# A softmax's division moved from the probabilities to the attention output, as a row that goes through DRAM

## The chip, the core and the metric

The kernel runs on one core of one Trainium2 chip, in one launch. The core has five engines with queues of their own: TensorE (PE: matmul; PEld: its weight loads), VectorE (DVE), ScalarE (ACT), GpSimd (POOL) and SyncE (SP), on whose queue nearly all DMAs are issued. An engine runs its queue in order; between engines, semaphores say when an operand is there or a buffer free. The metric is the time of one execution in microseconds, the median of several runs.

## The reference, cut to what matters

One decoder layer for a sequence of 512 tokens and a width of 1024: a SwiGLU block, then gated linear attention ("GLA") beside forgetting attention ("FoX"), then another SwiGLU block. The change lies in FoX: 16 heads of 64 columns, a causal softmax over 512 keys with a decay F in the logits.

```python
logf = jax.nn.log_sigmoid((f_b + b_f).astype(f32)).transpose(0, 2, 1)
F = jnp.cumsum(logf, axis=-1)
    s = jnp.einsum('bhqd,bhkd->bhqk', qi, k).astype(jnp.float32) * scale
    s = s + Fi[..., None] - F[:, :, None, :]
    s = jnp.where(kpos[None, :] <= qpos[:, None], s, -jnp.inf)
    p = jax.nn.softmax(s, axis=-1)
    return jnp.einsum('bhqk,bhkd->bhqd', p.astype(v.dtype), v)
merged = jax.nn.sigmoid(gate_a) * (o_a @ w_pa) + jax.nn.sigmoid(gate_b) * (o_b @ w_pb)
```

All of it is float32. The kernel gets this precision by cutting operands into two rounded halves (hi and lo, type fp32r) and adding three products of halves.

## The kernel before

The FoX stage works on eight pairs of heads (p = 0 to 7; e is the head within a pair; the two heads take 64 partitions each where a tile holds both). The loop over p (L990 to L1009) is written in this order: fox_soft(p), fox_scores(p + 1), transposes of p (fox_turn), output product of p (fox_out), and then evacuate(), which makes the operands of a later pair's scores out of matrix products. In a pair:

- fox_scores: SP loads a row of F for each head, broadcast to 128 partitions (L872); GpSimd prepares the decay and the mask (L876, L878); TensorE makes, for each of four blocks of 128 queries and each head, a score product in two parts (L890, L891); VectorE adds the decay and takes the row maxima (L894).
- fox_soft: the maxima are negated (L901), ScalarE takes the exponentials with their row sums (L903), VectorE the sums' reciprocals (L905), and each block of queries is multiplied by its reciprocal, one for each partition (L907: four instructions a head, of 128 to 512 columns).
- fox_turn: TensorE transposes the probabilities in blocks of 128 x 128 (L919), ScalarE copies them out (L921).
- fox_out: 16 products with the values (L930) give the output in PSUM with the 64 columns of each head on the partitions and the 512 queries in the columns; hilo (L208 to L210) rounds it into the high half on ScalarE (L209) and subtracts for the low half on VectorE (L210).
- evacuate: qk_parts (L743 to L763) makes the halves of queries and keys for the scores of a later pair out of two finished products: on ScalarE L755, L757 and L761, on VectorE L756, L758 and L760, for each head.

Beside that, TensorE is kept busy with the steps of Fill (L660 to L763): projections of the layer's input (L203), whose weights come in blocks. A block is loaded by SP into one of four buffers "raw" (L151), rounded on ScalarE into a buffer "whi" (L166), and its remainder is taken on VectorE into a buffer "wlo" (L167). There are five buffers each of whi and wlo, used in turn: the cast into one waits for the last product that read what was in it. The load of a step is written four steps ahead of its products.

The order of each engine's queue isn't the written one: a scheduler of the framework sorts all instructions by its own estimates. So an edit in one place can move instructions of other lines.

Of the kernel before, what the change touches and what calls it, by code (L numbers as in the profile page):

```python
# [8 lines left out]
F32 = mybir.dt.float32  # L9
# [4 lines left out]
ALU = mybir.AluOpType  # L14

P = 128
T = 512
D = 1024
NT = T // P
# [21 lines left out]
def tile_hybrid_layer(  # L41
# [4 lines left out]
    nc = tc.nc  # L46
# [6 lines left out]
    dr = ctx.enter_context(tc.tile_pool(name="dr", bufs=1, space=bass.MemoryType.DRAM))  # L53
# [5 lines left out]
    def nm(s):  # L59
        uid[0] += 1  # L60
        return f"{s}_{uid[0]}"

    def unit(dt=F32, shape=(P, 512)):
        return sb.tile(list(shape), dt, tag="u", bufs=NU, name=nm("u"))

    def tmp(shape=(P, 512), dt=F32):
        return sb.tile(list(shape), dt, tag="t2", bufs=NTMP, name=nm("t2"))
# [4 lines left out]
    def acc(shape=(P, 512)):  # L72
        return pm.tile(list(shape), F32, tag="mm", name=nm("mm"))
# [134 lines left out]
    def hilo(hi, lo, src, eng=None):  # L208
        nc.scalar.copy(hi, src)  # L209
        (eng or nc.vector).tensor_tensor(lo, src, hi.bitcast(F32), ALU.subtract)  # L210
# [447 lines left out]
    halves = (slice(0, 64), slice(64, P))  # L658
# [199 lines left out]
    def s_at(u, i):  # L858

        return (u[1][:, 384:512], u[2], u[1][:, 0:384], u[0])[i]  # L860

    def p_at(u, j):

        return (u[0], u[1][:, 0:384], u[2], u[1][:, 384:512])[j]
# [30 lines left out]
                                               ALU.add, ALU.max, nmx[e][:, i:i + 1])  # L895
        return S, nmx, rs

    def fox_soft(state):
        S, nmx, rs = state
        for e in range(2):  # L900
            nc.vector.tensor_scalar(nmx[e], nmx[e], -1.0, None, ALU.mult)  # L901
            for i in range(NT):
                nc.scalar.activation(s_at(S[e], i), s_at(S[e], i), AF.Exp, bias=nmx[e][:, i:i + 1],  # L903
                                     accum_out=rs[e][:, i:i + 1])
            nc.vector.reciprocal(rs[e], rs[e])  # L905
            for i in range(NT):
                nc.vector.tensor_scalar(s_at(S[e], i), s_at(S[e], i), rs[e][:, i:i + 1], None, ALU.mult)  # L907

    def fox_turn(state):
        S = state[0]  # L910
# [14 lines left out]
    def fox_out(p, PT):  # L925
        po = acc()
        for j in range(NT):
            for e in range(2):
                h = 2 * p + e
                nc.tensor.matmul(po[64 * e:64 * e + 64, j * P:T], vb[j][h // 8][:, (h % 8) * 64:(h % 8 + 1) * 64],  # L930
                                 p_at(PT[e], j), start=j == 0, stop=j == NT - 1)
        o = (unit(F32R), unit(F32R))
        hilo(o[0], o[1], po)
        ob.append(o)

    def sig_tanh(ps):
# [43 lines left out]
    def evacuate():  # L980
        while late:
            late.pop(0)()
# [4 lines left out]
    st = [fox_scores(0, *fqk[0], lambda: F.run(1))]  # L987
    evacuate()
    F.run(1)
    for p in range(8):  # L990
        fox_soft(st[p])
        if p < 7:
            F.run(1)
            st.append(fox_scores(p + 1, *fqk[p + 1], lambda: F.run(1) if p == 6 else None))
        if p < 6:
            F.until(marks[p + 2] - 1)
        else:
            F.run(2 if p == 6 else 3)
        PT = fox_turn(st[p])
        F.run(1)  # L1000
        fox_out(p, PT)
        evacuate()
        if p == 5:
            ra2 = tmp()
            tc.keep_in_program_order(nc.sync.dma_start(ra2[0:16], w_a2))
            wa2, fill_wa2 = stacked((0, 1, 0))
            fill_wa2(ra2[0:16])
        if p < 7:
            F.run(1)  # L1009
# [281 lines left out]
```

## Time and profile before

| | us |
|---|---|
| median of three runs (1421.54 to 1423.88) | 1421.57 |
| the profiled execution | 1425.45 |
| its span in the trace | 1423.4 |
| TensorE matmuls busy in the span | 1361.4 (96%) |
| VectorE busy | 910.4 (64%) |
| ScalarE busy | 595.5 (42%) |
| GpSimd busy | 206.6 (15%) |

The mean granted clock of TensorE over the span is 0.992 of full speed. The FoX stage lies between 480 and 660 us of the span. Busy time says how long an engine works, not whether anyone waits for it: the views that answer this are the waits of an engine (who ended its idle time), the engines in order of time, and the chain of work that ended last. In lines of the timeline, the bracket at the end gives the idle time just ahead and the instruction that ended it.

### The profile page before, as it was taken

To read this page: it belongs to the slowest core of one execution; us is meant where nothing else is said; L and a number is where in the kernel's file an instruction comes from. 1 tells how busy PE (TensorE), PEld (TensorE's weight loads), DVE (VectorE), ACT (ScalarE), POOL (GpSimd) and SP (SyncE) were. 2 spreads that over 40 slices of the span, in tenths; PEclk is the share of its full clock that TensorE was granted. 3 is DMA by queue.
4 is the path that set the end of the run, shared out by engine and by line. 5 is a ranking of instruction groups with operands and counts; after the bars stand their busy time and mean duration, and the time that the engine had idled before them with its cause. 6 is when DMAs were issued, how large, how long until landed. Compare 5 with 4: busy or idle time off the path is not lost.

```text
span 1423.4 us, 19497 instructions
## 1 busy us (share of the span) xinstructions
PE 1361.4 (96%) x7485; PEld 1146.4 (81%) x7485; DVE 910.4 (64%) x1410; ACT 595.5 (42%) x1026; POOL 206.6 (15%) x328
## 2 busy tenths in 40 slices
PE   4899999999999999999999999999999999999998
PEld 3699899888877867777888887787878999987886
DVE  6888678685266689762745546538577877866222
ACT  6444444223154476663723333332355444433221
POOL 6200000000050644340110202100050000000001
PEclk8999999999999999999999999999999999999999
DMA  9413233597336755322232232125631332346431
GB/s 322 150 62 112 82 104 110 179 290 265 103 107 182 226 163 167 94 71 78 90 117 75 60 87 62 60 74 160 210 119 45 119 119 75 104 134 196 130 118 59
DMA packets 164089, 180.84 MB, mean 127 GB/s; under 512 B 9226, under 2 KB 128118, under 8 KB 163996
## 3 DMA queue, kind: packets, MB, share of 16 engines
q1 hardware_dynamic: 163564, 178.81, 40.2%
q8 instruction: 59, 0.97, 0.3%
q10 hardware_dynamic: 432, 0.79, 0.2%
q14 instruction: 34, 0.28, 0.1%
HBM read 173.25 MB, written 6.32 MB: 126 GB/s over the span
## 4 chain that ended last, share of the span: by engine, by line
PE 71%; DVE 15%; DMA 6%; ACT 3%; issue 3%; POOL 2%; SPq 0%; DVEq 0%; POOLq 0%; ACTq 0%
PE mm L203 47%; PE mm L394 11%; PE mm L456 7%; DVE wlo L167 5%; DMA raw<-in_w_gu_dram 3%; PE aux L1108 1%; DMA u<-in_w_ada_dram 1%; DVE u L210 1%; DVE t L473 1%; ACT whi L166 1%; DMA raw<-in_w_ada_dram 1%; PE aux L919 1%; PE mm L930 1%; DVE u L907 1%; DVE raw L444 1%
## 5 line engine op out<-in xcount | busy, mean ns | idle before, releaser
L166 ACT CAST whi<-raw 128x1024 fp32r<-128x1024 f32 x262 | 273.3, 1050 | 516.7 <-PE mm L203 261.8
L167 DVE TENSOR_TENSOR wlo<-raw,whi 128x1024 fp32r<-128x1024 f32 x260 | 323.1, 1248 | 247.6 <-ACT whi L166 244.1
L203 PE MATMUL mm<-whi,u 128*128 128x512 f32 x1216 | 392.1, 398 | 1.7 <-DVE t L367 1.5
L203 PE MATMUL mm<-u,whi 128*128 128x512 f32 x896 | 289.9, 402 | 0.8 <-DVE u L1135 0.8
L456 PE MATMUL mm<-u,whi 128*128 128x256 f32 x1568 | 279.3, 281 | 10.6 <-DVE t L473 10.6
L203 PEld LDWEIGHTS mm<-whi,u 128*128 128x128 f32 x1216 | 228.2, 188 | 54.9 <-ACT u L209 1.7
L456 PEld LDWEIGHTS mm<-u,whi 128*128 128x128 f32 x1568 | 239.8, 188 | 13.9 <-DVE t L473 13.2
L203 PE MATMUL mm<-wlo,u 128*128 128x512 f32 x608 | 240.3, 395 | 1.0 <-DVE wlo L167 1.0
L456 PE MATMUL mm<-u,wlo 128*128 128x256 f32 x784 | 219.0, 280 | 0.0
L203 PEld LDWEIGHTS mm<-u,whi 128*128 128x128 f32 x896 | 167.3, 189 | 39.3 <-DVE u L1135 1.2
L394 PE MATMUL mm<-u,whi 128*128 128x512 f32 (+1 forms) x576 | 168.5, 380 | 11.0 <-ACT u L209 9.9
L203 PE MATMUL mm<-u,wlo 128*128 128x512 f32 x448 | 178.6, 399 | 0.0
L456 PEld LDWEIGHTS mm<-u,wlo 128*128 128x128 f32 x784 | 147.3, 188 | 0.0
L203 PEld LDWEIGHTS mm<-wlo,u 128*128 128x128 f32 x608 | 114.2, 188 | 28.8 <-DVE wlo L167 1.3
L394 PEld LDWEIGHTS mm<-u,whi 128*128 128x128 f32 x576 | 105.4, 191 | 35.1 <-ACT u L209 13.2
L394 PE MATMUL mm<-u,wlo 128*128 128x512 f32 (+1 forms) x288 | 105.4, 375 | 0.0
L203 PEld LDWEIGHTS mm<-u,wlo 128*128 128x128 f32 x448 | 84.7, 189 | 19.7
L321 POOL TENSOR_SCALAR sm<-ss 128x1 f32<-128x1 f32 x12 | 2.3, 190 | 642.9 <-ACT jk L328 642.9
L224 DVE SCALAR_TENSOR_TENSOR t<-raw,csil,t 128x512 f32<-128x512 f32 x98 | 74.0, 756 | 10.0 <-DMA raw<-in_w_ada_dram 7.8
L394 PEld LDWEIGHTS mm<-u,wlo 128*128 128x128 f32 x288 | 55.3, 192 | 10.3
L209 ACT CAST u<-t 128x256 fp32r<-128x256 f32 (+1 forms) x94 | 40.8, 454 | 43.5 <-DVE t L523 23.0
L876 POOL TENSOR_SCALAR u<-t,Ft 128x128 f32<-128x128 f32 (+1 forms) x64 | 44.3, 702 | 90.5 <-DMA t<-Fd 67.1
(197 smaller groups left out, 1381.1 us busy)
## 6 DMA issues: line engine op xcount, KB each, us to landing
raw<-in_w_gu_dram SPq DMA_DIRECT2D x88, 512.0 KB, 3.9
raw<-in_w_in_dram SPq DMA_DIRECT2D x64, 512.0 KB, 3.8
raw<-in_w_dn_dram SPq DMA_DIRECT2D x44, 512.0 KB, 5.2
raw<-in_w_ada_dram SPq DMA_DIRECT2D x64, 256.0 KB, 3.7
raw<-in_w_ada_dram SPq DMA_DIRECT2D x24, 512.0 KB, 5.2
u<-in_w_ada_dram SPq DMA_DIRECT2D x32, 256.0 KB, 6.3
raw<-in_w_in_dram SPq DMA_DIRECT2D x20, 256.0 KB, 2.8
t<-Fd SPq DMA_DIRECT2D x16, 256.0 KB, 5.1
```

Of the source, the lines that this page charges most:

```text
L166: nc.scalar.copy(hi, raw)
L167: (eng or nc.vector).tensor_tensor(lo, raw, hi.bitcast(F32), ALU.subtract)
L203: nc.tensor.matmul(ps, a[i], b[j], start=first and n == 0, stop=last and n == 2)
L209: nc.scalar.copy(hi, src)
L210: (eng or nc.vector).tensor_tensor(lo, src, hi.bitcast(F32), ALU.subtract)
L224: nc.vector.scalar_tensor_tensor(a, raw[:, j, :], csil[:, k:k + 1], a, ALU.mult, ALU.add)
L394: nc.tensor.matmul(p_[:, ts], w_[k][i][:, cs], hs[k][e][:, ts], start=ks[0] == 0 and n == 0, stop=ks[-1] == KD - 1 and n == 3 * len(ks) - 1)
L444: nc.vector.tensor_tensor(a12, a12, a11, ALU.subtract)
L456: nc.tensor.matmul(ps[:, j], *((h_[:, js], w_) if self.turned else (w_[:, js], h_)), start=first and k + j + m == 0, stop=k == 3 and m == ...
L473: nc.vector.tensor_tensor(o, ps, a, ALU.add)
L876: nc.gpsimd.tensor_scalar(s_at(s, i), fb[:, 0:n], -1.0, Ft[:, i, h:h + 1], ALU.mult, ALU.add)
L907: nc.vector.tensor_scalar(s_at(S[e], i), s_at(S[e], i), rs[e][:, i:i + 1], None, ALU.mult)
```

## The change

The exponentials are no longer multiplied by the reciprocals (L907 is gone). The transposes and the products with the values take them as they are. The division is made on the output: there, a query is a column, so the reciprocals are needed as a row. They are stored to DRAM as one row of 512 for each head (512 pieces of four bytes, out of a tile of 128 x 4) and loaded again, broadcast to the 64 partitions of that head. VectorE multiplies the product in PSUM by this tile and writes the result over it in SBUF (L940 of after); hilo then reads this.

```diff
--- before.py
+++ after.py
@@ -895,7 +895,10 @@
                                                ALU.add, ALU.max, nmx[e][:, i:i + 1])
         return S, nmx, rs
 
-    def fox_soft(state):
+    Rd = dr.tile([16, T], F32, name="Rd")
+    rows_ = []
+
+    def fox_soft(p, state):
         S, nmx, rs = state
         for e in range(2):
             nc.vector.tensor_scalar(nmx[e], nmx[e], -1.0, None, ALU.mult)
@@ -903,8 +906,12 @@
                 nc.scalar.activation(s_at(S[e], i), s_at(S[e], i), AF.Exp, bias=nmx[e][:, i:i + 1],
                                      accum_out=rs[e][:, i:i + 1])
             nc.vector.reciprocal(rs[e], rs[e])
-            for i in range(NT):
-                nc.vector.tensor_scalar(s_at(S[e], i), s_at(S[e], i), rs[e][:, i:i + 1], None, ALU.mult)
+
+            nc.sync.dma_start(Rd[2 * p + e].rearrange("(i p) -> p i", p=P), rs[e])
+        row = unit()
+        for e in range(2):
+            nc.sync.dma_start(row[halves[e]], Rd[2 * p + e].partition_broadcast(64))
+        rows_.append(row)
 
     def fox_turn(state):
         S = state[0]
@@ -930,7 +937,8 @@
                 nc.tensor.matmul(po[64 * e:64 * e + 64, j * P:T], vb[j][h // 8][:, (h % 8) * 64:(h % 8 + 1) * 64],
                                  p_at(PT[e], j), start=j == 0, stop=j == NT - 1)
         o = (unit(F32R), unit(F32R))
-        hilo(o[0], o[1], po)
+        nc.vector.tensor_tensor(rows_[p], po, rows_[p], ALU.mult)
+        hilo(o[0], o[1], rows_[p])
         ob.append(o)
 
     def sig_tanh(ps):
@@ -988,7 +996,7 @@
     evacuate()
     F.run(1)
     for p in range(8):
-        fox_soft(st[p])
+        fox_soft(p, st[p])
         if p < 7:
             F.run(1)
             st.append(fox_scores(p + 1, *fqk[p + 1], lambda: F.run(1) if p == 6 else None))
```

With that the scheduler's order changes from about 480 us to the end of the FoX stage; outside it, TensorE's order is the same. Three places follow, of before and of after. In the names, a number at the end marks one buffer's use; line numbers of after are three to eight higher (L921 is L928, L905 is L908).

SP, in pair 0, before: the F row of a later head (t) between weight loads (raw).

```order
L268 DMA raw_4892<-in_w_ada_dram 128x2x256 x2
L268 DMA raw_4897<-in_w_ada_dram 128x2x256 x2
L268 DMA raw_4902<-in_w_ada_dram 128x2x256 x2
L872 DMA t_842_4729<-Fd 128x512
L268 DMA raw_4907<-in_w_ada_dram 128x2x256 x2
L151 DMA raw_4946<-in_w_in_dram 128x8x128
L151 DMA raw_5026<-in_w_in_dram 128x8x128
```

The same in after:

```order
L268 DMA raw_4899<-in_w_ada_dram 128x2x256 x2
L910 DMA Rd<-sm_4349 128x4x1
L910 DMA Rd<-sm_4364 128x4x1
L913 DMA u_4478<-Rd 64x512
L872 DMA t_844_4725<-Fd 128x512
L913 DMA u_4478<-Rd 64x512
L268 DMA raw_4904<-in_w_ada_dram 128x2x256 x2
L151 DMA raw_4940<-in_w_in_dram 128x8x128
L151 DMA raw_5020<-in_w_in_dram 128x8x128
```

The two stores, which wait for the reciprocals of pair 0, and the two loads of the row (u_4478) have come between the weight loads; t_844 is issued between the two loads of the row.

ScalarE, ahead of the scores of pair 4, before: whi casts, the output's rounding (L209), then for each head L755, L757, L761.

```order
L166 CAST whi_5411<-raw_5409 128x1024
L209 CAST u_5105<-mm_5096 128x512
L755 CAST u_5111<-mm_4913 64x512
L757 ACTIVATE u_5109<-mm_4912 64x512
L761 COPY u_5111<-u_5113 64x512
L755 CAST u_5112<-mm_4913 64x512
L757 ACTIVATE u_5110<-mm_4912 64x512
L761 COPY u_5112<-u_5114 64x512
L166 CAST whi_5491<-raw_5489 128x1024
```

The same in after:

```order
L166 CAST whi_5401<-raw_5399 128x1024
L209 CAST u_5099<-u_4937 128x512
L755 CAST u_5106<-mm_4910 64x512
L757 ACTIVATE u_5104<-mm_4909 64x512
L761 COPY u_5106<-u_5108 64x512
L755 CAST u_5107<-mm_4910 64x512
L166 CAST whi_5481<-raw_5479 128x1024
L757 ACTIVATE u_5105<-mm_4909 64x512
L761 COPY u_5107<-u_5109 64x512
L928 COPY u_5263<-aux_5266 128x512
L928 COPY u_5264<-aux_5272 128x512
```

The last cast of a weight block (whi_5491 before, whi_5481 after) has moved from behind both heads' operands to ahead of the second head's L757, and two copies of transposes (L928) stand behind.

VectorE at the same place, before:

```order
L905 RECIPROCAL sm_4993<-sm_4993 128x4
L907 TENSOR_SCALAR u_4982<-u_4982,sm_4993 128x128
L907 TENSOR_SCALAR u_4983<-u_4983,sm_4993 128x256
L907 TENSOR_SCALAR u_4982<-u_4982,sm_4993 128x384
L907 TENSOR_SCALAR u_4981<-u_4981,sm_4993 128x512
L167 TENSOR_TENSOR wlo_5242<-raw_5239,whi_5241 128x1024
L210 TENSOR_TENSOR u_5106<-mm_5096,u_5105 128x512
L756 TENSOR_TENSOR u_5113<-mm_4913,u_5111 64x512
L758 SCALAR_TENSOR_TENSOR u_5109<-mm_4912,u_5109 64x512
L760 COPY u_5113<-u_5111 64x512
L286 SCALAR_TENSOR_TENSOR scc_3823<-aux_5129,cols 128x2
L287 TENSOR_TENSOR shc_3822<-aux_5129,cols 128x2
```

And in after:

```order
L167 TENSOR_TENSOR wlo_5234<-raw_5231,whi_5233 128x1024
L940 TENSOR_TENSOR u_4937<-mm_5090,u_4937 128x512
L286 SCALAR_TENSOR_TENSOR scc_3823<-aux_5124,cols 128x2
L287 TENSOR_TENSOR shc_3822<-aux_5124,cols 128x2
L288 TENSOR_TENSOR scc_3823<-scc_3823,cols 128x2
L167 TENSOR_TENSOR wlo_5402<-raw_5399,whi_5401 128x1024
L210 TENSOR_TENSOR u_5100<-u_4937,u_5099 128x512
L756 TENSOR_TENSOR u_5108<-mm_4910,u_5106 64x512
L758 SCALAR_TENSOR_TENSOR u_5104<-mm_4909,u_5104 64x512
L760 COPY u_5108<-u_5106 64x512
L756 TENSOR_TENSOR u_5109<-mm_4910,u_5107 64x512
L760 COPY u_5109<-u_5107 64x512
```

The four multiplies are gone, the new one (L940) stands behind the first weight remainder, and two more remainders stand between: wlo_5402 ahead of L210, wlo_5482, of the block whose cast moved, ahead of the second head's L758 (the row that follows is L758 with u_5105).

TensorE at the scores of pair 4, before (u_5111 to u_5114 and u_5109, u_5110 are the operands made above):

```order
L890 MATMUL mm_5207<-u_5111,u_5109 128x128
L203 MATMUL mm_5163<-u_3616,whi_4948 128x512
L891 MATMUL mm_5207<-u_5113,u_5109 128x128
L203 MATMUL mm_5163<-u_3617,whi_4948 128x512
L203 MATMUL mm_5163<-u_3616,wlo_4949 128x512
L203 MATMUL mm_5163<-u_3618,whi_4948 128x512
L203 MATMUL mm_5163<-u_3619,whi_4948 128x512
L203 MATMUL mm_5163<-u_3618,wlo_4949 128x512
L203 MATMUL mm_5163<-u_3620,whi_4948 128x512
L890 MATMUL mm_5210<-u_5112,u_5110 128x128
L891 MATMUL mm_5210<-u_5114,u_5110 128x128
L890 MATMUL mm_5215<-u_5111,u_5109 128x256
```

And in after (u_5104 to u_5109 are the operands):

```order
L203 MATMUL mm_5155<-u_3621,whi_4942 128x512
L203 MATMUL mm_5155<-u_3620,wlo_4943 128x512
L890 MATMUL mm_5199<-u_5106,u_5104 128x128
L891 MATMUL mm_5199<-u_5108,u_5104 128x128
L926 MATMUL aux_5266<-ident,u_4961 128x128
L926 MATMUL aux_5266<-ident,u_4962 128x128
L926 MATMUL aux_5266<-ident,u_4961 128x128
L926 MATMUL aux_5266<-ident,u_4960 128x128
L926 MATMUL aux_5272<-ident,u_4962 128x128
L926 MATMUL aux_5272<-ident,u_4961 128x128
L926 MATMUL aux_5272<-ident,u_4960 128x128 x2
L890 MATMUL mm_5202<-u_5107,u_5105 128x128
```

Before, products of L203 stand between the first and the second head's first scores; after, they have all been done ahead of the scores, the last read of whi_4942 being the first row (whi_5481 takes its buffer), and eight transposes (L926) of the pair before stand between.

## Rows read from the trace of the kernel before

**Rows 1.** Stretches: us, PE, PEld, DVE, ACT, POOL busy (instructions), granted clock, DMA share, GB/s.

```profile
480.00:660.00 180.00, 174.82 (x906) 134.55 (x905) 127.95 (x334) 109.94 (x256) 71.96 (x134) 0.99 0.42 125
620.00:630.00 10.00, 9.71 (x38) 7.96 (x39) 7.00 (x22) 3.29 (x9) 2.55 (x4) 0.83 0.33 100
```

**Rows 2.** TensorE's waits, 480 to 660 us: us in total, times, longest.

```profile
PE mm L890 <- DVE u L758: 4.0, 3, 1.8
PE mm L890 <- DVE sm L894: 0.5, 1, 0.5
PE mm L891 <- DVE u L760: 0.4, 2, 0.2
```

**Rows 3.** Timeline of PE: start, us, operation, idle ahead and its releaser.

```profile
499.81 0.30 PE L890 MATMUL mm<-u,u 128*128 128x128 f32 x1 [1.19 <-DVE u L758]
...
620.11 0.30 PE L890 MATMUL mm<-u,u 128*128 128x128 f32 x1 [1.82 <-DVE u L758]
```

**Rows 4.** Groups by line and shape, L907: busy us, mean ns, idle ahead.

```profile
L907 DVE TENSOR_SCALAR u<-u,sm 128x128 f32<-128x128 f32 x16 | 5.0, 312 | 0.4
L907 DVE TENSOR_SCALAR u<-u,sm 128x256 f32<-128x256 f32 x16 | 6.8, 426 | 0.0
L907 DVE TENSOR_SCALAR u<-u,sm 128x384 f32<-128x384 f32 x16 | 8.1, 509 | 0.0
L907 DVE TENSOR_SCALAR u<-u,sm 128x512 f32<-128x512 f32 x16 | 8.9, 559 | 0.0
```

**Rows 5.** Chain that ended last, 480 to 680 us, shares by line.

```profile
by line: PE mm L203 44.8%; PE aux L919 5.8%; PE mm L930 5.8%; DVE u L907 5.1%; issue 4.2%; PE mm L890 3.6%; PE mm L891 3.6%; ACT u L903 3.1%; DVE u L758 2.4%; DVE u L756 2.3%; DVE u L894 2.2%; DVE wlo L167 2.2%; ACT u L921 1.5%; DVE u L210 
```

**Rows 6.** Timeline of DVE ahead of the scores of pair 3.

```profile
533.54 2.25 DVE L907 TENSOR_SCALAR u<-u,sm 128x128 f32<-128x128 f32 x4
535.71 1.48 DVE L167 TENSOR_TENSOR wlo<-raw,whi 128x1024 fp32r<-128x1024 f32 x1
...
537.72 0.67 DVE L756 TENSOR_TENSOR u<-mm,u 64x512 fp32r<-64x512 f32 x1
```

**Rows 7.** Timeline of ACT in the same place.

```profile
527.23 1.07 ACT L921 COPY u<-aux 128x512 f32<-128x512 f32 x2
...
533.17 1.06 ACT L166 CAST whi<-raw 128x1024 fp32r<-128x1024 f32 x1
```

**Rows 8.** Groups by line and shape: L758 and L167 of 480 to 660, L209 of the span.

```profile
L758 DVE SCALAR_TENSOR_TENSOR u<-mm,u 64x512 fp32r<-64x512 f32 x16 | 11.0, 688 | 0.8 <-ACT u L757 0.4
...
L167 DVE TENSOR_TENSOR wlo<-raw,whi 128x1024 fp32r<-128x1024 f32 x20 | 25.5, 1280 | 17.9 <-ACT whi L166 16.5 <-DMA raw<-in_w_in_dram 1.4
...
L209 ACT CAST u<-u 128x512 fp32r<-128x512 f32 x20 | 11.9, 618 | 32.7 <-DVE u L605 23.7 <-DVE u L407 4.1 <-DVE u L405 2.8
```

**Rows 9.** Timeline of PE: output products of pairs 0 and 1.

```profile
510.80 2.37 PE L930 MATMUL mm<-u,u 128*64 128x512 f32 x16
...
531.63 2.37 PE L930 MATMUL mm<-u,u 128*64 128x512 f32 x16
```

**Rows 10.** Timeline of ACT behind the operands of pair 4.

```profile
558.55 0.62 ACT L761 CAST u<-u 64x512 fp32r<-64x512 f32 x1 [0.31 <-DVE u L756]
562.03 1.06 ACT L166 CAST whi<-raw 128x1024 fp32r<-128x1024 f32 x1 [2.87 <-PE mm L203]
```

**Rows 11.** Chain that ended last: eight transposes.

```profile
526.70 0.87 PE aux L919 x8
```

**Rows 12.** DMA issues: operation, count, KB each, median us to landing.

```profile
t<-Fd SPq DMA_DIRECT2D x16, 256.0 KB, 5.1
...
Fd<-u SPq DMA_DIRECT2D x1, 32.0 KB, 2.5
...
sm<-in_b_f_dram SPq DMA_DIRECT2D x1, 0.1 KB, 3.3
```

**Rows 13.** Timeline of DVE in pair 0.

```profile
502.66 0.17 DVE L905 RECIPROCAL sm<-sm 128x4 f32<-128x4 f32 x1
```

**Rows 14.** Timeline of DVE ahead of the scores of pair 7.

```profile
617.24 1.28 DVE L167 TENSOR_TENSOR wlo<-raw,whi 128x1024 fp32r<-128x1024 f32 x1
```

## The prediction

> **What bounds the kernel now.** I read the table of stretches first. In the stretch that the change touches, 480 to 660 us, TensorE is busy 174.82 of 180 us, VectorE 127.95, ScalarE 109.94 [rows 1]. So TensorE sets the end there, and work that leaves VectorE is worth only what TensorE waits for. The second view, TensorE's waits in that stretch, names these: 4.0 us in three waits for the query parts that L758 makes, 0.5 us for a row maximum of L894, 0.4 us for L760 [rows 2]. Together that is 4.9 us out of 180. The third view, TensorE in order of time, shows the two largest: 1.19 us at 499.81 (scores of pair 1) and 1.82 us at 620.11 (pair 7) [rows 3], both times the second head's first score product, which waits for its operands; the last of the three is then 4.0 - 1.19 - 1.82 = 1.0 us, at pair 3. Behind the wait at 620.11 the granted clock of 620 to 630 us is 0.83 instead of 1.00 [rows 1], part of the time on the lower of its two levels, 1.2 instead of 2.4 GHz; 10 us at 0.83 cost 10 x 0.17 = 1.7 us, if the wait is what brought the clock down. So the whole change can return at most 4.9 + 1.7 = 6.6 us, however much it takes from VectorE.
>
> **The change part by part.** (1) The 64 multiplies of L907 leave: 16 each of four widths, 5.0 + 6.8 + 8.1 + 8.9 = 28.8 us of VectorE [rows 4]. They stand between the softmax's reciprocals and the transposes, and the chain of waits does carry L907 for 5.1% of its 200 us from 480 to 680 [rows 5], some 10 us. But that chain names whatever was last at each step, with TensorE's own queue close behind it; by [rows 2] TensorE sees at most 4.9 us of it.
>
> (2) What decides are the scores of a pair, since their operands (L755 to L761) are made right after the attention output of the pair two before is cut into its two halves. At pair 3 the trace shows this chain on VectorE: four multiplies of L907 from 533.54, a weight remainder (L167) at 535.71, the output's remainder (L210), L756 at 537.72 [rows 6]. After, this begins with L167. Its rounded half is cast on ScalarE from 533.17 for 1.06 us [rows 7], behind the exponentials; L167 takes 1.28 [rows 8], to 535.5. Then the new multiply by the row, which no row shows; its nearest is L758, which also reads a matrix product 512 columns wide and takes 688 ns [rows 8]: 0.7, to 536.2. Only then ScalarE rounds the output (618 ns for one from SBUF [rows 8]), to 536.8, a cast that ran beside L907 before; L210 with 0.7, and L756 starts at 537.5 instead of 537.72. So **28.8 us less of VectorE moves this chain by only 0.2 us**, since the multiply and the cast now stand in a row in it. Bounds: if L167 came behind L756, this would start 534.0 + 0.7 + 0.6 + 0.7 = 536.0, 1.7 us sooner, 534.0 being the end of the output's product (531.63 + 2.37 [rows 9]); if a second weight remainder stands between, as in the order's rows of VectorE before the scores of pair 4, it starts 1.28 - 0.6 - 0.2 = 0.5 us later than now. In all eight new multiplies cost 8 x 0.69 = 5.5 us, so VectorE's whole busy time falls by 28.8 - 5.5 = 23.3 us.
>
> (3) The transposes no longer wait for L907. In the order of after, the first eight transposes of the odd pairs therefore stand between the scores of the following pair, and two of ScalarE's copies, 1.07 us at 527.23 among the exponentials [rows 7], go ahead of these, into time in which ScalarE waits. The exponentials of pairs 2, 4 and 6, and with them the chain of (2) for the scores of pairs 3, 5 and 7, then end 1.1 us earlier. At pair 3 this makes 0.2 + 1.1 = 1.3 us, within the bound of 1.7 that the output's product sets: more than the 1.0 us of waiting.
>
> (4) The same move brings a new coupling, shown by the order's rows for ScalarE, VectorE and TensorE at the scores of pair 4. The cast of a later weight block, whi, has moved ahead of L757 of the second head. It fills a slot that is free only when TensorE has done the last product that reads the old block, and in after this product stands right before the scores. In before that cast stood behind L761: it starts at 562.03 after 2.87 us of waiting for a product of L203, and nobody needs it, the L761 ahead of it having started at 558.55 [rows 10]. After, the second head's scores wait for TensorE's own product, then the cast of 1.06 [rows 10], then a remainder L167 of 1.28, which stands ahead of L758 on VectorE, then L758, 0.69 [rows 8]: 3.0 us. What covers it on TensorE are the eight transposes, 0.87 us [rows 11], and some 0.4 us of short products: 1.3. New wait at pair 4: 3.0 - 1.3 = **1.7 us**. Before the scores of pair 2 the cast alone stands ahead of L757: 1.06 + 0.62 (as L761 [rows 10]) + 0.69 - 1.3 = 1.1 us; before those of pair 6 it stands ahead of L761 only: 1.06 + 0.62 - 1.3 = 0.4 us. Bounds: 0, where the slot is free earlier, to twice these.
>
> (5) The rows' way through DRAM: 16 stores of 128 x 4 and 16 loads of 64 x 512 on SP's queue, none of which exists before. Bounds for a store from the nearest rows: 2.5 us (Fd<-u) to 3.3 (sm<-in_b_f, sixteen four-byte pieces) [rows 12]; for a load, half of t<-Fd's 256 KB, 2.5, to its whole 5.1 [rows 12]. The tightest is pair 0: its second reciprocal is done at 502.66 + 0.17 = 502.83 [rows 13], so the row is there between 507.8 and 511.2. It is needed when the output product of pair 0 ends, 510.80 + 2.37 = 513.2 [rows 9]. Cover 2.0 to 5.4 us, so its cost is nothing; I take the small cover, since the pieces are small. The other pairs' reciprocals come a pair ahead of their output. Waiting on SP's queue behind a store are t<-Fd and weight loads; of the idle time before L167 only 1.4 us is put down to a weight load [rows 8], so a store of a few us ahead is hidden. Without the cover a late row holds the multiply, and behind it on VectorE the next pair's reciprocal, L167, L210 and L756 to L760, for which TensorE's scores wait.
>
> The Trainium skill's page "DMA: Bandwidth & Descriptors", section "Specifications", asks for at least 512 bytes a transfer, below which the DMA engine reads, modifies and writes. Each store here is 512 pieces of four bytes, so by it (5) would be the place to lose. No row of before shows such a store; the sixteen four-byte pieces that it shows are reads. The sum doesn't use the rule; what it would do is the last rival.
>
> (6) Pair 7. A remainder of L167 (617.24, 1.28 us [rows 14]) leaves from between the two heads' L756, and (3) moves the chain up; the lateness of pairs 4 and 6 uses up part of the wait of 1.82 at 620.11 in any case. It shrinks by 0.5 to 1.8 us; I take 1.2.
>
> **The sum on TensorE's path.** Pair 1's wait at 499.81 has no L907 ahead of it: 0. Pair 2: now 0.5 + 0.2 for L894 and L760 [rows 2], after 1.1: +0.4. Pair 3: -1.0. Pair 4: +1.7. Pair 5, which doesn't wait now: 0. Pair 6: +0.4. Pair 7: -1.2. Row: 0. Together 0.4 - 1.0 + 1.7 + 0.4 - 1.2 = **+0.3 us**. The profiled execution took 1425.45 us and becomes 1425.75; it is 3.9 us above the median of the runs, and the difference carries over: 1421.57 + 0.3, **1421.9 us**. About 0.2%, 2.8 us, is what a measurement of this kernel can tell from no change.
>
> **Rivals.** *Relief reaches TensorE.* If (4) is smaller than I read it, because the cast's slot comes free early enough, all waits of [rows 2] but that at 499.81 go, 3.7 us, and the clock's 1.7 too: -5.4, 1416.2 us. For it: the chain carries 10 us of L907 [rows 5]. Against it: the order shows the new wait. *The new coupling costs more.* Each wait of 1.7 us can bring the clock down as at 620 us: if those of pairs 2 and 4 each cost 1.7 on top, and pair 7 gives back only 0.5: 0.3 + 3.4 + 0.7 = +4.4, 1426.0 us. For it: 1.82 us of idling was followed by 0.83. Against it: 1.19 us at 499.81 was not, the whole stretch being at 0.99 [rows 1]. *The row comes late.* If 512 four-byte stores take over 3.3 + 2.0 = 5.3 us to land, pair 0 waits; at three times the 3.3, 9.9, the row is 4.6 us late, the scores of pair 2 start that much later, and pair 3's may lose 2 more: +5 to +7, 1427 to 1429 us. It decides from 5.3 us on. *The multiplies don't go away*: excluded, no L907 is in the order of after.
>
> **How the numbers follow.** Forecast 0.47 (1418.7 to 1424.4, likeliest 1421.9); relief 0.19; coupling 0.20; late row 0.14. So faster by over 0.2% 0.19, within it 0.47, slower 0.34. The range goes from 1417.0 (most of the first rival lies below) to 1428.5 (part of the last lies above), which leaves out 0.2.
>
> **What would show it.** VectorE's busy time of the whole span falls by some 23 us, TensorE's doesn't change. Among TensorE's waits there is one of 1 to 2 us for L758 at the scores of pairs 2 and 4 each, none at pair 3, a short one at pair 7. The new multiply waits for no transfer at any pair or, if the last rival is right, for microseconds at pair 0; the store's time to landing says which. The forecast is wrong if the clock drops at more than one place, if the new multiply takes much over 0.7 us, or if the stage's end shifts by more than 3 us.

## The result, and the profile after

The changed kernel takes **1441.62 us**, median of four runs (1439.33 to 1443.64), against 1421.71 us for the kernel before on the same chip: ratio 1.0135, 95% interval 1.0122 to 1.0148. It is 19.9 us slower; 1421.9 us was forecast, with a range of 1417.0 to 1428.5. The profiled execution took 1442.24 us, with a span of 1440.5.

VectorE did lose its work. In the page's first part, VectorE falls from 910.4 to 893.9 us, 16.5 less; added up instruction by instruction it is 22.7 less (the busy time counts the overlap of neighbouring instructions once):

```profile
PE 1370.6 (95%) x7485; PEld 1153.6 (80%) x7485; DVE 893.9 (62%) x1354; ACT 596.5 (41%) x1026; POOL 204.7 (14%) x328
```

The stretch of the FoX stage has grown. Stretches as in [rows 1] (us, PE, PEld, DVE, ACT, POOL busy, granted clock, DMA share, GB/s):

```profile
480.00:700.00 220.00, 201.33 (x996) 156.02 (x995) 118.80 (x287) 122.54 (x270) 69.83 (x134) 0.95 0.54 120
520.00:540.00 20.00, 16.13 (x81) 12.39 (x82) 11.71 (x30) 12.50 (x31) 3.79 (x8) 0.83 0.72 83
540.00:560.00 20.00, 17.10 (x76) 13.93 (x75) 13.36 (x33) 9.29 (x21) 8.36 (x16) 0.83 0.72 171
560.00:580.00 20.00, 14.26 (x75) 10.72 (x74) 12.96 (x27) 10.84 (x22) 5.58 (x8) 0.89 0.65 115
```

Before, TensorE was busy 174.82 of the 180 us of [rows 1], at 0.99. Now there are three stretches of 20 us with 14 to 17 us of TensorE, at 0.83 to 0.89. Look at the two columns at the end: from 520 to 540 us the DMA engines are busy for 0.72 of the time and move 83 GB/s; from 540 to 560 us the same 0.72 moves 171. Busy engines that move little are the first sign.

The waits of TensorE, 480 to 700 us (in total, times, longest), answer [rows 2]:

```profile
PE mm L890 <- DVE u L758: 16.8, 9, 6.3
PE mm L890 <- DVE u L760: 0.9, 1, 0.9
PE mm L890 <- ACT u L761: 0.7, 1, 0.7
```

4.0 us in three waits have become 16.8 in nine. The two longest, in the timeline of TensorE (compare [rows 3]):

```profile
523.71 0.45 PE L890 MATMUL mm<-u,u 128*128 128x128 f32 x1 [6.31 <-DVE u L758]
...
577.93 0.45 PE L890 MATMUL mm<-u,u 128*128 128x128 f32 x1 [4.23 <-DVE u L758]
```

They stand at the scores of pairs 2 and 4. Ahead of the first stands VectorE's queue, here its timeline in pair 0:

```profile
501.14 0.18 DVE L908 RECIPROCAL sm<-sm 128x4 f32<-128x4 f32 x1 [2.00 <-ACT u L906]
...
516.64 0.69 DVE L940 TENSOR_TENSOR u<-mm,u 128x512 f32<-128x512 f32 x1 [5.31 <-DMA u<-Rd]
```

And ScalarE's timeline in the same place:

```profile
519.35 1.04 ACT L166 CAST whi<-raw 128x1024 fp32r<-128x1024 f32 x1 [7.52 <-DMA raw<-in_w_in_dram]
```

The reciprocal of pair 0's second head is done at 501.3, but the new multiply starts only at 516.64, after 5.31 us of waiting for the row (u<-Rd): 501.3, a store's 10.5 us and a load's 5.1 (both below) make 516.9. And ScalarE's cast waits as well: it has been idle 7.52 us, and what it waits for is a weight block.

Of the two, the cast ends last. The multiply is done at 517.33, but the remainder of that block stands between it and L210, L756 and L758 on VectorE, and it waits for the cast:

```profile
520.43 1.23 DVE L167 TENSOR_TENSOR wlo<-raw,whi 128x1024 fp32r<-128x1024 f32 x1 [1.82 <-ACT whi L166]
```

Why the block is late, SP's queue shows:

```profile
499.16 2.55 SPq L910 DMA_DIRECT2D Rd<-sm  x2
508.27 0.51 SPq L913 DMA_DIRECT2D u<-Rd  x1
...
512.54 1.04 SPq L151 DMA_DIRECT2D raw<-in_w_in_dram  x2
```

From 501.71 to 508.27 SP issues nothing: the row's load (L913) is next in its queue and waits for the store. The weight load behind it is issued at 512.54 and lands 6.7 us later. Between 480 and 700 us the row loads wait on SP's queue for their stores eight times, 32.0 us in all, up to 7.3. So a late store delays more than its own row: it delays whatever stands behind the row's load.

The groups of these two, 480 to 700 us (busy, mean, idle ahead and what ended it):

```profile
L166 ACT CAST whi<-raw 128x1024 fp32r<-128x1024 f32 x23 | 24.0, 1050 | 37.5 <-DMA raw<-in_w_in_dram 15.4 <-PE mm L203 12.6 <-issue 4.1
...
L940 DVE TENSOR_TENSOR u<-mm,u 128x512 f32<-128x512 f32 x8 | 5.5, 685 | 7.8 <-DMA u<-Rd 5.5 <-PE mm L937 2.3
```

15.4 us of the casts' idle time ends with a weight load. In before there is no such part in that group's row:

```profile
L166 ACT CAST whi<-raw 128x1024 fp32r<-128x1024 f32 x26 | 26.8, 1054 | 28.6 <-PE mm L203 18.0 <-issue 5.6 <-PE mm L890 3.9
```

The DMA issues (count, KB each, median us to landing) point at the cause; they answer [rows 12]:

```profile
u<-Rd SPq DMA_DIRECT2D x16, 128.0 KB, 5.1
...
Rd<-sm SPq DMA_DIRECT2D x16, 2.0 KB, 10.5
...
Fd<-u SPq DMA_DIRECT2D x1, 32.0 KB, 2.7
```

A store of 2 KB in 512 pieces takes **10.5 us** to land, a store of 32 KB 2.7. I had bounded it at 2.5 to 3.3.

### The profile page after: what moved, and what is told of

Its sections match the earlier page's. It is cut to its first block, busy times and chain, and to the rows that moved or that the text cites. A ratio compares the mean times of both kernels' runs of the same rounds, so it can differ in the third digit from the quotient of the medians.

```text
span 1440.5 us, 19524 instructions
## 1 busy us (share of the span) xinstructions
PE 1370.6 (95%) x7485; PEld 1153.6 (80%) x7485; DVE 893.9 (62%) x1354; ACT 596.5 (41%) x1026; POOL 204.7 (14%) x328
## 4 chain that ended last, share of the span: by engine, by line
PE 66%; DVE 15%; DMA 9%; ACT 4%; issue 3%; POOL 2%; SPq 0%; DVEq 0%; POOLq 0%; ACTq 0%
PE mm L203 42%; PE mm L394 11%; PE mm L456 8%; DVE wlo L167 4%; DMA raw<-in_w_in_dram 3%; DMA raw<-in_w_gu_dram 3%; PE aux L1116 1%; ACT whi L166 1%; DMA raw<-in_w_dn_dram 1%; DMA raw<-in_w_ada_dram 1%; DVE u L210 1%; DVE t L473 1%; DVE t L224 1%; DMA Rd<-sm 1%; DVE raw L444 1%
## 5 line engine op out<-in xcount | busy, mean ns | idle before, releaser
L167 DVE TENSOR_TENSOR wlo<-raw,whi 128x1024 fp32r<-128x1024 f32 x260 | 323.2, 1248 | 257.9 <-ACT whi L166 254.5
L203 PE MATMUL mm<-whi,u 128*128 128x512 f32 x1216 | 391.4, 397 | 1.7 <-ACT u L209 1.5
L203 PE MATMUL mm<-u,whi 128*128 128x512 f32 x896 | 288.3, 401 | 0.8 <-DVE u L1143 0.8
L203 PEld LDWEIGHTS mm<-whi,u 128*128 128x128 f32 x1216 | 228.2, 188 | 55.7 <-ACT u L209 1.7
L203 PE MATMUL mm<-wlo,u 128*128 128x512 f32 x608 | 241.4, 397 | 1.6 <-DVE wlo L167 1.6
L203 PEld LDWEIGHTS mm<-u,whi 128*128 128x128 f32 x896 | 166.9, 189 | 39.6 <-DVE u L1143 1.2
L203 PE MATMUL mm<-u,wlo 128*128 128x512 f32 x448 | 178.6, 399 | 0.0
L203 PEld LDWEIGHTS mm<-wlo,u 128*128 128x128 f32 x608 | 114.2, 188 | 29.3 <-DVE wlo L167 2.8
L203 PEld LDWEIGHTS mm<-u,wlo 128*128 128x128 f32 x448 | 84.8, 189 | 19.8
L394 PEld LDWEIGHTS mm<-u,wlo 128*128 128x128 f32 x288 | 55.9, 194 | 10.6
L209 ACT CAST u<-t 128x256 fp32r<-128x256 f32 (+1 forms) x94 | 40.8, 454 | 43.5 <-DVE t L523 22.9
L876 POOL TENSOR_SCALAR u<-t,Ft 128x128 f32<-128x128 f32 (+1 forms) x64 | 40.6, 645 | 121.3 <-DMA t<-Fd 102.2
```

The lines of the kernel that those rows point to most:

```text
L167: (eng or nc.vector).tensor_tensor(lo, raw, hi.bitcast(F32), ALU.subtract)
L203: nc.tensor.matmul(ps, a[i], b[j], start=first and n == 0, stop=last and n == 2)
L394: nc.tensor.matmul(p_[:, ts], w_[k][i][:, cs], hs[k][e][:, ts], start=ks[0] == 0 and n == 0, stop=ks[-1] == KD - 1 and n == 3 * len(ks) - 1)
L876: nc.gpsimd.tensor_scalar(s_at(s, i), fb[:, 0:n], -1.0, Ft[:, i, h:h + 1], ALU.mult, ALU.add)
```

## The experiments

The question was which part costs the 19.9 us: the new order of the queues, the row that comes late, or the stores themselves, by what they do to other transfers. Each kernel was run four to ten times and is compared with the kernel before, run on the same chip beside it (median 1423.49 us for e1 to e4, 1423.42 for e5 to e8, 1422.65 for e9 to e12). The last column is the median of the landings that the trace recorded.

| kernel | median us | over before | ratio, 95% interval | store's landing us |
|---|---|---|---|---|
| after | 1441.62 | +19.9 | 1.0135 (1.0122 to 1.0148) | 10.5 |
| e1_no_trip | 1423.53 | 0.0 | 1.0003 (0.9993 to 1.0013) | no store |
| e2_stores_only | 1436.46 | +13.0 | 1.0096 (1.0072 to 1.0120) | 9.9 |
| e3_before_stores | 1443.14 | +19.7 | 1.0139 (1.0122 to 1.0155) | 10.4 |
| e4_16byte_pieces | 1426.65 | +3.2 | 1.0023 (1.0010 to 1.0036) | 2.5 |
| e5_128_pieces | 1429.62 | +6.2 | 1.0043 (1.0027 to 1.0058) | 8.6 |
| e6_spread | 1423.41 | 0.0 | 1.0005 (0.9993 to 1.0018) | 2.1 |
| e7_other_queue | 1441.97 | +18.6 | 1.0129 (1.0111 to 1.0148) | 10.6 |
| e8_pinned_no_trip | 1424.78 | +1.4 | 1.0013 (1.0000 to 1.0026) | no store |
| e9_turned_row | 1433.64 | +11.0 | 1.0069 (1.0046 to 1.0092) | not recorded |
| e10_spacing_16 | 1423.30 | +0.7 | 1.0011 (0.9998 to 1.0025) | 3.0 |
| e11_trip_spread | 1426.42 | +3.8 | 1.0029 (1.0015 to 1.0043) | 2.5 |
| e12_trip_close | 1439.52 | +16.9 | 1.0123 (1.0095 to 1.0151) | 12.3 |

### Without the way through DRAM: e1_no_trip

```diff
-            nc.sync.dma_start(Rd[2 * p + e].rearrange("(i p) -> p i", p=P), rs[e])
-        row = unit()
-        for e in range(2):
-            nc.sync.dma_start(row[halves[e]], Rd[2 * p + e].partition_broadcast(64))
-        rows_.append(row)
...
-        nc.vector.tensor_tensor(rows_[p], po, rows_[p], ALU.mult)
+        rows_.append(unit())
+        nc.vector.tensor_tensor(rows_[p].rearrange("q (i c) -> q i c", c=P), po.rearrange("q (i c) -> q i c", c=P),
+                                ones.unsqueeze(1).to_broadcast([P, NT, P]), ALU.mult)
```

> The change without its way through DRAM: no stores, no row loads; the output product is multiplied by a tile of ones that is there all along (the division is left out). The multiplies L907 are gone and the queues' order is that of after but for small shifts: the later cast whi stands ahead of the second head's L757 or L761 at pairs 2, 4 and 6. Theory 'trip' (the row's transfers cost the time): within 3 us of before, 1419 to 1425 us. Theory 'order' (the new coupling of the cast and the chain of multiply and cast cost it): 1435 us or more, with waits for L758 of several us at pairs 2 and 4.

Measured: 1423.53 us, as before. Its order is that of after but for small shifts. So the change without its transfers costs and gains nothing that these times can tell, and the theory "order" has fallen. TensorE's waits, 480 to 700 us:

```profile
PE mm L890 <- DVE u L758: 3.7, 3, 2.3
PE mm L890 <- ACT u L761: 2.2, 3, 0.9
PE aux L921 <- ACT u L923: 0.5, 2, 0.3
```

The timeline of TensorE at the scores of pairs 2, 4, 6 and 7:

```profile
520.70 0.33 PE L890 MATMUL mm<-u,u 128*128 128x128 f32 x1 [0.61 <-ACT u L761]
...
561.38 0.44 PE L890 MATMUL mm<-u,u 128*128 128x128 f32 x1 [2.32 <-DVE u L758]
...
602.01 0.33 PE L890 MATMUL mm<-u,u 128*128 128x128 f32 x1 [0.67 <-ACT u L761]
...
619.90 0.30 PE L890 MATMUL mm<-u,u 128*128 128x128 f32 x1 [0.24 <-DVE u L758]
...
622.13 0.33 PE L890 MATMUL mm<-u,u 128*128 128x128 f32 x1 [0.88 <-ACT u L761]
```

The relief and the new waits that the prediction set against each other are both there: pair 3 doesn't wait any more, pair 7 waits less, and pairs 2, 4 and 6 have new waits at the second head's operands, 2.32 us at pair 4.

### The stores alone: e2_stores_only and e3_before_stores

e2 is e1 with the line of the stores put back; no row is loaded. On TensorE, ScalarE and VectorE its queues hold the same instructions in the same order as those of e1. e3 is the kernel before with this line added behind the reciprocals; on TensorE, ScalarE, VectorE and GpSimd its queues hold the same instructions in the same order as those of before:

```diff
             nc.vector.reciprocal(rs[e], rs[e])
+            nc.sync.dma_start(Rd[2 * p + e].rearrange("(i p) -> p i", p=P), rs[e])
```

> As e1_no_trip, but with the 16 stores of 512 four-byte pieces left in; nobody reads what they store (no row loads, the division is left out). Theory 'late row' (VectorE's queue held at the multiply by a late row is the cost): like e1_no_trip, within 2 us. Theory 'queue' (transfers behind a store on the same DMA queue, weight loads above all, come later): 5 us or more above e1_no_trip, with ScalarE's casts of weights waiting for their loads.

> The kernel before, with its 64 multiplies, and only the 16 stores of reciprocals in four-byte pieces added; nobody reads them. Theory 'late row': as before, 1421.7 us within 2. Theory 'queue': 5 us or more above before, whatever the order of the engines' queues is.

Measured: +13.0 and +19.7 us, where nobody waits for a store's data. So the late row isn't the main cause: the stores alone make the kernel before as slow as the changed one. The group of the casts in e2:

```profile
L166 ACT CAST whi<-raw 128x1024 fp32r<-128x1024 f32 x23 | 23.9, 1051 | 35.1 <-PE mm L203 12.6 <-DMA raw<-in_w_in_dram 11.5 <-issue 4.1
```

And in e3:

```profile
L166 ACT CAST whi<-raw 128x1024 fp32r<-128x1024 f32 x23 | 24.0, 1054 | 43.1 <-PE mm L203 19.6 <-DMA raw<-in_w_in_dram 12.6 <-issue 5.6
```

The whole stretch of e2:

```profile
480.00:700.00 220.00, 204.12 (x1021) 159.18 (x1021) 123.43 (x293) 128.41 (x279) 74.29 (x137) 0.96 0.52 113
```

And of e1:

```profile
480.00:700.00 220.00, 213.38 (x1067) 166.50 (x1066) 133.30 (x311) 138.32 (x289) 75.35 (x139) 0.98 0.39 114
```

The same 113 and 114 GB/s keep the DMA engines busy for 0.52 of the time instead of 0.39, and 11.5 us of the casts' idle time ends with a weight load. That is a single wait, ahead of the scores of pair 2, where TensorE then waits 9.18 us. The weight loads themselves (L151, 480 to 680 us, from issue to landing) take up to 14.7 us in e2:

```profile
DMA to landing us min/median/max: 2.9/5.4/14.7
```

And in e6, a kernel of the next section that has the same stores and the same order, up to 5.3:

```profile
DMA to landing us min/median/max: 2.9/4.6/5.3
```

What the stores cost differs with the order of the queues: 13.0 us in that of e2, 19.7 in that of before. Which loads are under way beside a store is the likely reason; no run singles it out.

### What makes a store slow: e4 to e6 and e10

Four edits of the store's layout, of which the lines that differ are shown. e4 is the whole change with 128 pieces of 16 bytes; the other three are e2 with another target, and their queues on TensorE, ScalarE and VectorE hold the same instructions in the same order as those of e1 and e2.

```diff
 e4: a partition's four reciprocals side by side; the multiply reads with a stride
     (pq: a view as four blocks of 128 columns; dv: a new buffer for the result)
-            nc.sync.dma_start(Rd[2 * p + e].rearrange("(i p) -> p i", p=P), rs[e])
+            nc.sync.dma_start(Rd[2 * p + e].rearrange("(p i) -> p i", i=NT), rs[e])
+        nc.vector.tensor_tensor(pq(dv, P), pq(po, P), rows_[p].rearrange("q (c i) -> q i c", i=NT), ALU.mult)
 e5: one of the four columns
+            nc.sync.dma_start(Rd[2 * p + e, 0:P].rearrange("(i p) -> p i", p=P), rs[e][:, 0:1])
 e6: 64 bytes from piece to piece, Rd 16 times as wide (e10: w=4, 16 bytes, Rd four times)
+            nc.sync.dma_start(Rd[2 * p + e].rearrange("(i p w) -> p i w", p=P, w=16)[:, :, 0:1], rs[e].unsqueeze(2))
```

> The whole change with the DRAM row laid out so that each partition's four reciprocals lie side by side: a store is 128 pieces of 16 bytes instead of 512 of four; the multiply reads the row with a stride. Theory 'pieces' (a store's time goes with its number of pieces): landing falls from 10.5 to 4 us or less, and the time to 1422 to 1430 us. Theory 'small writes' (any write under 512 bytes is slow to be confirmed, however many): landing stays at 8 us or more and the time at 1436 us or more.

> As e2_stores_only (nobody reads the stores, no division), but each store takes only one of the four columns: 128 pieces of four bytes. Theory 'number of pieces': landing 2 to 4 us, time within 3 us of e1_no_trip. Theory 'piece size' (four bytes is slow whatever the number): landing 8 us or more and 5 us or more above e1_no_trip.

> As e2_stores_only, with all 512 pieces of four bytes, but laid out 64 bytes apart in DRAM instead of side by side. Theory 'number of pieces': landing about 10 us as before and time about 1436 us. Theory 'neighbours' (pieces that write into the same stretch of DRAM wait for one another): landing 4 us or less and time within 3 us of e1_no_trip.

> As e6_spread (nobody reads the stores, no division), 512 pieces of four bytes, but 16 bytes apart instead of 64. Four pieces fall into the same 64 bytes, as in e4_16byte_pieces. If the landing goes with the number of pieces that fall into the same 64 bytes: 2.5 to 4 us, time within 3 us of e1_no_trip. If any two neighbours within 64 bytes cost the whole hold: 8 us or more, time about 1436 us.

Measured, by the row of the DMA issues of e4:

```profile
Rd<-sm SPq DMA_DIRECT2D x16, 2.0 KB, 2.5
```

Of e5:

```profile
Rd<-sm SPq DMA_DIRECT2D x16, 0.5 KB, 8.6
```

Of e6:

```profile
Rd<-sm SPq DMA_DIRECT2D x16, 2.0 KB, 2.1
```

Of e10:

```profile
Rd<-sm SPq DMA_DIRECT2D x16, 2.0 KB, 3.0
```

- The number of pieces isn't it: 512 pieces land in 2.1 us when they lie 64 bytes apart (e6), and 128 take 8.6 us when they lie side by side (e5).
- The size of a piece isn't it either: four bytes are slow in e5 and fast in e6. Alone, e4 would have looked like proof of "pieces"; it changed number and size at once.
- It is the **neighbourhood**: four-byte pieces side by side are slow, 16 bytes apart they are nearly free, 64 bytes apart free. e6 is e2 with another address for each piece and nothing else, and the 13.0 us are gone. Sixteen pieces in the same 64 bytes are slow (e2), four aren't (e10); distances between 4 and 16 bytes weren't tried.

e5 costs 6.2 us, under half of e2's, although its landing is nearly as long. Its share of DMA engine time over the same stretch is smaller too. In e6 this share is:

```profile
480.00:700.00 220.00, 213.68 (x1081) 166.39 (x1080) 135.98 (x317) 139.95 (x290) 75.56 (x139) 1.00 0.41 114
```

And in e5:

```profile
480.00:700.00 220.00, 208.31 (x1037) 162.00 (x1036) 126.16 (x300) 131.84 (x281) 78.21 (x138) 0.97 0.47 112
```

0.41 for e6, 0.47 for e5, 0.52 for e2, at 112 to 114 GB/s each.

The whole change in the layout of e4 is still 3.2 us slower than before (interval 1.0010 to 1.0036). Its multiply, which reads the row in steps of 16 bytes, takes 1068 ns instead of 685, and whether the rest comes from there wasn't followed up:

```profile
L942 DVE TENSOR_TENSOR u<-mm,u 128x512 f32<-128x512 f32 x8 | 8.5, 1068 | 2.3 <-PE mm L937 2.3
```

### Which transfers are held: e7_other_queue

```diff
-            nc.sync.dma_start(Rd[2 * p + e].rearrange("(i p) -> p i", p=P), rs[e])
+            nc.scalar.dma_start(Rd[2 * p + e].rearrange("(i p) -> p i", p=P), rs[e])
```

> As e2_stores_only, with the stores issued on ScalarE's DMA queue instead of SP's. Theory 'behind on the queue' (only transfers of the same queue are held): weight loads land in their usual 3 to 5 us and the time falls to 1424 to 1428 us, ScalarE losing 16 issues of some 0.4 us. Theory 'engines held' (the 16 DMA engines themselves are held, whatever queue): time stays at 1433 us or more, with casts waiting for weight loads.

Measured: +18.6 us, no better than on SP's queue. The weight loads, all still on SP's queue, are held just the same. The store among the DMA issues, now on ScalarE's queue:

```profile
Rd<-sm ACTq DMA_DIRECT2D x16, 2.0 KB, 10.6
```

And the group of the casts:

```profile
L166 ACT CAST whi<-raw 128x1024 fp32r<-128x1024 f32 x23 | 24.1, 1048 | 37.6 <-DMA raw<-in_w_in_dram 15.4 <-PE mm L203 14.5 <-issue 4.1
```

So the stores hold transfers of another queue too, not only what stands behind them on their own. The DMA engines are busy as in e2, 0.53 of the time at 112 GB/s, so it is most likely the engines that are held. (ScalarE's own queue has another order here, since it issues the stores; the 15.4 us of waiting for weight loads are what the verdict rests on.)

### All transfers, without the dependence: e11_trip_spread and e12_trip_close

Both have the stores, the row loads and the multiply of after, but the loads read rows of F, so they needn't wait for a store (the division by the row sums is left out). They differ in the store's address alone, and the order of their queues is the same.

```diff
-            nc.sync.dma_start(row[halves[e]], Rd[2 * p + e].partition_broadcast(64))
+            nc.sync.dma_start(row[halves[e]], Fd[2 * p + e].partition_broadcast(64))
```

> All transfers of the change but without the dependence: stores spread 64 bytes apart into a tensor that nobody reads, row loads from rows of F instead (the multiplier is the wrong one), so the loads needn't wait for a store. If stores and loads as such are free once the pieces don't neighbour: within 2 us of e1_no_trip, 1422 to 1426 us.

> As e11_trip_spread, with the stores of after (512 pieces side by side); the queues' order is the same as in e11_trip_spread. The difference to it is the engines held; the difference from here to after is the wait of the row for its store. Theory: 1433 to 1439 us, that is 10 to 15 us over e11_trip_spread, and 3 to 8 us under after.

Measured: 1426.42 and 1439.52 us. The stretch of e11:

```profile
480.00:700.00 220.00, 212.58 (x1066) 165.83 (x1065) 133.98 (x312) 138.91 (x290) 75.51 (x139) 0.98 0.45 123
```

Of e12:

```profile
480.00:700.00 220.00, 200.79 (x1014) 156.23 (x1014) 120.91 (x292) 126.70 (x276) 75.25 (x137) 0.97 0.61 120
```

At 123 and 120 GB/s, engines busy 0.45 and 0.61. The difference, 13.1 us, is the neighbourhood again, now with all other parts of the change in place. The 3.8 us of e11 over before are more than the 2 I expected; its order isn't e1's, and loads and order weren't told apart. From e12 to after 19.9 - 16.9 = 3.0 us are left. The intervals of the two ratios overlap, and e12's order on ScalarE and VectorE isn't that of after, so what the row's wait for its store costs isn't shown by the times. In the trace of after it stands in two places: the 5.31 us of L940 in pair 0, and the 32.0 us in which the row loads keep SP's queue from issuing. No run separates these two; row loads on another queue would.

### Two attempts at a better kernel: e8_pinned_no_trip and e9_turned_row

e8 is e1 with dependences that keep casts and remainders of weight blocks written after L761 behind it (newest() is the instruction just written; pinned holds the last L761 and L760):

```diff
         nc.scalar.copy(hi, raw)
+        i = newest()
         (eng or nc.vector).tensor_tensor(lo, raw, hi.bitcast(F32), ALU.subtract)
+        j = newest()
+        if pinned:
+            after_inst(i, pinned[0])
+            if not eng:
+                after_inst(j, pinned[1])
```

> e1_no_trip with one more rule: casts and remainders of weight blocks written after a pair's score operands (L755 to L761) may not be put ahead of them on ScalarE and VectorE. The division is left out. Theory 'coupling' (part 4 of the prediction's sum costs what the order says): the waits for L758 and L761 at the scores fall from 6 us to under 2 and the time to 1417 to 1421 us. Rival: the casts, now later, come too late for the products behind the scores, and TensorE waits for them instead: 1423 us or more.

Measured: 1424.78 us, no gain. The waits at the scores fell from 3.7 + 2.2 us to 3.9 us in two:

```profile
PE mm L902 <- DVE u L767: 3.9, 2, 2.7
PE aux L933 <- ACT u L935: 1.1, 2, 0.9
```

Nothing waits for L761 any more, but two waits for the second head's operands stay (L767 and L902 are L758 and L890 there), 2.7 us at pair 1 and 1.2 at pair 7, and the waits for copies of transposes have grown from 0.5 to 1.1 us; I had expected under 2 us in all. What the casts' later place costs elsewhere wasn't followed up.

e9 is the whole change with a row that TensorE turns, so that a store has 8 pieces of 512 bytes (r8 holds the reciprocals of both heads, 128 x 8):

```diff
-            nc.sync.dma_start(Rd[2 * p + e].rearrange("(i p) -> p i", p=P), rs[e])
+        tp = aux((P, P))
+        nc.tensor.transpose(tp[:8, :], r8, ident)
+        rt = unit()[:8, 0:P]
+        nc.vector.tensor_copy(rt, tp[:8, :])
+        nc.sync.dma_start(Rd[2 * p:2 * p + 2].rearrange("e (i c) -> (e i) c", c=P), rt)
```

> The whole change, with the two heads' 128 x 8 reciprocals turned on TensorE into 8 x 128 first, so that the store of a pair is 8 pieces of 512 bytes; the row loads and the multiply are those of after. Theory 'neighbours': landing 2 to 3 us, no casts waiting for weight loads, time 1422 to 1427 us (the eight transposes, copies and another order of the queues may cost some 2 us). If another part of the trip (the loads, the multiply's wait) costs on its own: 1430 us or more.

Measured: 1433.64 us, 11.0 over before, against my expectation. The transfers don't show as the cause: the casts wait 0.9 us in all for weight loads, no multiply waits for its row. The groups of the casts and of the multiply (L945 there):

```profile
L166 ACT CAST whi<-raw 128x1024 fp32r<-128x1024 f32 x24 | 25.1, 1047 | 33.9 <-PE mm L203 23.6 <-issue 5.2 <-DVE wlo L167 3.3
...
L945 DVE TENSOR_TENSOR u<-mm,u 128x512 f32<-128x512 f32 x8 | 5.5, 684 | 2.1 <-PE mm L942 2.1
```

And TensorE's waits, 480 to 700 us:

```profile
PE mm L891 <- DVE u L758: 7.2, 5, 2.8
PE aux L931 <- DVE u L914: 1.3, 2, 1.1
PE mm L891 <- DVE u L760: 1.1, 1, 1.1
PE mm L203 <- DVE sm L895: 1.1, 3, 0.4
```

TensorE waits 7.2 us in five for L758 (L891 is L890 there), and the copy of the turned row (L914) holds transposes of the probabilities (L931) for 1.3 us. The scheduler has put casts ahead of the second head's L757 at pairs 2, 4 and 6, and exponentials between the operands of pair 2. These waits are 4 to 5 us longer than in e1, which doesn't make up 11; the rest is open. None of the runs points to a version that is faster than the kernel before: e1, the change without any transfer, is no faster.

## Why the prediction was wrong

- **What bounds the kernel.** Right. 23 us less work on VectorE bring nothing that shows by themselves (e1: 0.0 us, interval -1.0 to +1.9).
- **The multiply (2).** Right: 8 of 685 ns, forecast 688. The instructions of VectorE add up to 22.7 us less, forecast 23.3.
- **The relief (3) and the coupling (4).** Right in place and nearly in size, by e1, which has them without the transfers: pair 3 -1.0 us (forecast -1.0), pair 4 +2.3 (+1.7), pair 6 +0.7 (+0.4), pair 2 0.6 instead of 0.7 (1.1 instead of 0.7), pair 7 0.24 + 0.88 = 1.1 instead of 2.0, so -0.9 (-1.2). Their sum is -1.0 + 2.3 + 0.7 - 0.1 - 0.9 = +1.0; forecast +0.3; measured 0.0. That the sums lie so close is partly luck: single terms are off by up to 0.6 us and cancel, and 1 us is within the noise.
- **The row's way through DRAM (5): the step that failed.** I bounded the store's landing at 2.5 to 3.3 us, by a store of 2 KB pieces and a load of sixteen four-byte pieces, and called its cost nothing. It lands in 10.5 us. The upper bound came from a read, and neither row had small pieces written side by side. The threshold of 5.3 us fits: with 10.5 us pair 0's multiply waits, with the 2.5 of e4 it doesn't.
- **What the late landing costs.** The last rival had the right start (a landing of three times 3.3, 9.9 us) and priced only the wait of the multiply: +5 to +7, 1427 to 1429 us. By e12 that part is some 3 us, not shown clear of noise. What it left out is that the stores hold other transfers, those of another queue too (e7). "So a store of a few us ahead is hidden" holds for a store of a few us (e6: 2.1 us, cost 0.0), not for these, and the sentence looked only at what stands behind a store on SP's queue. It also passed over the row's load there, which waits for the store with weight loads behind it. Weight loads come late, the casts wait for them (15.4 us), and the operands of the scores stand behind the casts or their remainders, so TensorE waits. The neighbouring pieces alone cost 13 us where only the address differs (e2 - e6, e12 - e11). Of the 19.9 that leaves the 3.8 of e11 and the 3.0 from e12 to after, whose causes stay open. In after the late load also meets the coupling of (4): at pair 4, TensorE's wait of 4.23 us has in it a cast that waits for its load:

```profile
574.75 1.04 ACT L166 CAST whi<-raw 128x1024 fp32r<-128x1024 f32 x1 [2.13 <-DMA raw<-in_w_in_dram]
575.82 0.59 ACT L757 ACTIVATE u<-mm 64x512 fp32r<-64x512 f32 x1
```

  The coupling isn't needed for the loss, though: e3, in the order of before, loses 19.7 us.

- **The clock.** The stretches with the long waits have a granted clock of 0.83 to 0.89 (520 to 580 us), between its levels of 1.2 and 2.4 GHz, as the second rival feared. The prediction had TensorE's busy time unchanged; it rose from 1361.4 to 1370.6 us, part of that outside the stage. The waits of the stage that are shown grew from 4.9 to 18.4 us, by 13.5; the other 6.4 of the 19.9 are then, as an estimate, mostly slower matmuls. With the hold the slow clock goes too: e2 runs 480 to 700 us at 0.96, e6 at 1.00 (e1, without stores, at 0.98).
- **The rule on small pieces.** The Trainium skill's page "DMA: Bandwidth & Descriptors", section "Specifications", has the DMA engine read, modify and write below 512 bytes. That pointed at the right place, and I gave it 0.14. Size alone doesn't decide here: the four-byte pieces of e6 land in 2.1 us, those of e2 in 9.9, and they differ only in where they lie. Why neighbours are slow, no run here shows.

## What to carry to other kernels

Before a small store is called free, look at where its pieces land: a column scattered as neighbouring four-byte pieces is the dear layout, and moving each piece 16 bytes away or making it 16 bytes long takes most of the cost away (e10 +0.7 us, e4 +3.2, against +13.0 and +19.9). Price a new transfer not only by who waits for its data, but by what else the DMA engines have to carry at that time; an experiment that issues it with nobody waiting separates the two. And look at what stands behind a load that has to wait for its store: on a queue that runs in order, it waits too. A bound for a write wants a row of a write with the same pieces; where there is none, the bound is open above, and the rival deserves more than 0.14.

## What was not expected of the hardware

- Median landing of a store: 512 four-byte pieces side by side 9.9 to 12.3 us; 128 of them 8.6; 16 bytes apart 3.0; 64 bytes apart 2.1 (e6) and 2.5 (e11); 128 pieces of 16 bytes side by side 2.5.
- Other transfers beside them are held too, those of another queue included (e7), and the engines count as busy: 0.52 of the time in e2, 0.41 in e6, at 113 and 114 GB/s.
- The row in steps of 16 bytes made the multiply take 1068 instead of 685 ns (e4).
